# The scores of the attention take their PSUM banks from the tag with four banks instead of the one with two

## Chip, cores and metric

The kernel runs on one core of a Trainium2 chip. The metric is the device time of one execution in microseconds. Three runs of the kernel before gave a median of 1214.59 us (1214.19 to 1215.19). In what follows PE is TensorE, DVE is VectorE, ACT is ScalarE, POOL is GpSimd, and SP is the engine that issues most transfers.

## What is computed

Two layers of a hybrid backbone over 256 latent tokens and 256 context tokens, 1024 wide, in float32. Each layer has a mixer with four parallel branches (pooling, short convolution, attention, a bidirectional Mamba-2 SSD) between one input and one output projection. Then comes a SwiGLU FFN in layer 0 and a mixture of eight experts (MoE) in layer 1. The core of the reference, for one layer:

```python
sh1, sc1, gt1, sh2, sc2, gt2 = split(silu(c) @ w_ada[l] + b_ada[l])
h, hc = rmsnorm(x) * (1 + sc1) + sh1, rmsnorm(xc) * (1 + sc1c) + sh1c
...
o = concatenate([pool_mix(p_pool), short_conv_mix(p_conv),
                 na_attention(q, k, v, kc, vc, rpb), o_ssd])
x = x + gt1 * (o @ w_out[l])
...
def ctx_attention(q, k, v):
    s = jnp.einsum('bqhd,bkhd->bhqk', q, k) * (1.0 / math.sqrt(hd))
    p = jax.nn.softmax(s, axis=-1)
    return jnp.einsum('bhqk,bkhd->bqhd', p, v)
```

The attention has four heads of 64 channels. A latent token attends to latent tokens in a window (with a bias) and to all context tokens; a context token attends to context tokens alone. The context stream is needed out of layer 0 but not out of layer 1, so layer 1 computes the latent half alone.

## The kernel before

The kernel is one program of some 18,000 instructions. A scheduler in the framework decides the order in which each engine runs them. It simulates the program with its own costs (`TCARGS`, L21) and takes the order of the code as priority. Which PSUM bank a tile may have is one of its constraints, so a change of banks can reorder instructions far from the place where it is made. Each engine then works through its own order, and an instruction that waits holds up all that stand behind it on its engine.

PSUM has eight banks of 128 partitions by 512 float32. `PSB` (L25) shares them out to three tags, `g` with four banks, `s` with two and `m` with two. `ps(tag, name)` (L364) takes a tile of one bank from the rotation of its tag. The tag `g` serves the input projections (tiles `g_...`, also the groups of `G4`) and, while a mixer runs, the products `adaps` and `adao` of the modulation vectors. `s` serves the SSD branch (`gram`, `rowbc`, `inter`, `yps`) and `poolps`. `m` serves the transposes of `turn` (L750) and, before the change, the whole attention.

A weight of the projections is split on the way in: `raw` comes from memory, ACT writes its rounded high part `wh` (L284), and DVE the rest `wl` (L287). A projection tile `g_N` is a chain of products with `wh` and `wl` from the same bank. Most products are recorded at the helper's line, L342, so tiles are told apart by their names.

The attention (`attn`, L757) is a generator. Its units are (context or latent, head, half of the queries); layer 0 has 16 of them and layer 1 has 8. It is advanced by `NATT` units (4 in layer 0, 2 in layer 1) for each projection. For a pair of heads, `scores` makes two products of 64 rows of TensorE each, one head on rows 0 to 63, the other on rows 64 to 127, each into a bank of its own:

```python
for i in range(2):
    r = slice(64 * i, 64 * i + 64)
    both.append(self.ps(ATAGS[0], "attS"))
    ms.append(self.mm(both[i][:, :nk], self.qT[r, c, q0:q0 + P], self.kT[r, c, k0:k0 + nk]))
self.inorder(ms)
```

`nk` is 512 for latent queries and 256 for context queries. `stage1` is the softmax on ACT and DVE: for latent units a copy of the context half (L784), the bias `nab` added to the rest (`attsb`, L785), the maximum (L786), the exponential (L787), the reciprocal and the scaling of `attP` (L788, L789); context units go by L780 and L781 instead. `stage2` transposes the probabilities into a bank of tag `ATAGS[1]` (`attT`, L796) and copies them to `PT` on ACT (L797). `pv` multiplies them with the values into a bank of tag `ATAGS[2]` (`attO`), eight products of 64 columns of TensorE for a latent pair and four for a context pair, and `hilo` splits that into `omx` (L399, L400), an input of the output projection.

Other work stands in the same stretches. Pooling copies its projection to `pu` (L690), sums shifted copies on DVE (L696 to L711) and multiplies on TensorE (`poolps`). The SSD makes `decay` (ACT L972, DVE L991) and `xd` (L980) for the products `yps`, adds the `inter` products on DVE (L1006, L1010: `ysb`), gates with `zs` (L1013), normalises (L1015 to L1020) and transposes on TensorE (`ytr`, L1024).

Of the kernel before, what the change touches and what calls it, by code (L numbers as in the profile page):

```python
# [31 lines left out]
OSLOT = ("xst", "Bt", "nab", "zs", None, None, "BT", "CT")  # L32
ADAFILL = (0, 1, 0, 1, 0, 1, 0, 1, 0, 1, 0, 1, 0, 0, 0, 0, 0, 0, 1, 1, 0, 0, 0, 0, 0, 0, 0, 0, 0, 0, 0, 0, 0, 0, 0, 0, 0, 0, 0, 0, 1, 1, 1, 0, 0, 0, 0, 0, 0, 0, 0, 0, 0, 0, 0, 0, 0, 0, 0, 0, 0, 0)
NATT = ((4, 4, 4, 4, 4, 4, 4, 4, 4, 4, 4, 4, 4, 4, 4, 4), (2, 2, 2, 2, 2, 2, 2, 2, 2, 2, 2, 2, 2, 2, 2, 2))
ATAGS = 'mmm'
G4 = 'gggg'
ADAGROUPS = ((0, (4, 5, 6, 7)), (0, (8, 9)), (1, (0, 1)), (1, (4, 5, 6)))

# [217 lines left out]
class Kern:  # L256
# [500 lines left out]
    def attn(self, full):  # L757
        V, A = self.V, self.A

        def scores(ctx, c, qt):  # L760
# [5 lines left out]
# [4 lines that stand above are left out]
# [22 lines left out]
        def stage2(pr, pt, qt):  # L792
            n = pr.shape[-1] // P
            tp = self.ps(ATAGS[1], "attT")
            for c in range(n):
# [21 lines left out]
        def pv(ctx, c):  # L817
            op = self.ps(ATAGS[2], "attO")
            nk = 2 if ctx else 4
            kb = 2 if ctx else 0  # L820
            ms = []
            for k in range(nk):
                for h in (2 * c, 2 * c + 1):
                    r = 64 * (h % 2)
                    ms.append(self.mm(op[r:r + 64, :256], self.vt[:, kb + k, h * 64:h * 64 + 64], pts[ctx, h][:, k, :],
                                      start=k == 0, stop=k == nk - 1))
            self.inorder(ms)
            o0 = 256 * ctx
            self.hilo(self.out(4 + c), slice(o0, o0 + 256), op[:, :256])
# [1194 lines left out]
```

## Time and profile before

| | us |
|---|---|
| median of three runs | 1214.59 (1214.19 to 1215.19) |
| the profiled execution | 1213.07 |
| its span (first to last instruction) | 1211.3 |
| TensorE busy | 1165.6 (96%) |
| VectorE busy | 736.8 (61%) |
| ScalarE busy | 461.1 (38%) |

The stages follow one another: start, mixer of layer 0 (about 70 to 240 us, attention on TensorE from 128), FFN (about 275 to 660), mixer of layer 1 (about 660 to 805, attention from 731), MoE (to the end). A row of the timeline is a run of equal instructions on one engine: start, length, engine, line, operation, what it writes and reads, shape, and how many records it merges (one float32 product of the attention's scores has two). In brackets stands the idle time ahead of it, if there is one, and what ended it. A row's length includes an end that overlaps the next row, so what a run costs is read from the start of the next row.

### The profile page before, as it was taken

Reading aid. Unit: us, or ns where it says so; the run is one execution under the profiler, and the core shown is the slowest. Engines: PE = TensorE matmul, PEld = TensorE weight load, DVE = VectorE, ACT = ScalarE, POOL = GpSimd, SP = SyncE. Lnnn points to the kernel's source line nnn. Section 1 sums busy time; section 2 is a strip of 40 time slices with the busy share of each in tenths; the row PEclk is TensorE's granted clock in tenths of the full one; section 3 lists DMA queues with packets and bytes.
Section 4 is the critical chain, followed back from the end, with each engine's and each line's share of the span. In section 5 each row is a group of like instructions: output and inputs, shape, how many; then the busy total and the mean of one; then the engine's idle time right before and its main releaser. Section 6 shows DMA issues by size and latency. Waiting matters only on the chain. (4 is left out here: it accounts for less than half of the span.)

```text
span 1211.3 us, 17942 instructions
## 1 busy us (share of the span) xinstructions
PE 1165.6 (96%) x6601; PEld 831.0 (69%) x6601; DVE 736.8 (61%) x1612; ACT 461.1 (38%) x863; POOL 8.9 (1%) x30
## 2 busy tenths in 40 slices
PE   6999999999999999999999999988999999999994
PEld 3787676787788888888886897884467534446741
DVE  4554667347979756764336778644588524447942
ACT  4443453324322231232223555541276423435721
POOL 0000000000000000000000000000000000000000
PEclk9999999999999999999999999998999999999997
DMA  9635424229565443543223442276999999896984
GB/s 373 228 138 209 144 83 139 84 87 374 201 206 187 162 155 128 187 154 122 87 101 126 141 139 88 90 252 244 359 401 407 344 401 394 300 409 238 375 286 179
DMA packets 88752, 264.16 MB, mean 218 GB/s; under 512 B 8144, under 2 KB 24144, under 8 KB 88528
## 3 DMA queue, kind: packets, MB, share of 16 engines
q1 hardware_dynamic: 88080, 260.84, 59.1%
q0 software_dynamic: 576, 2.10, 0.5%
q8 instruction: 54, 0.88, 0.3%
q14 instruction: 42, 0.34, 0.1%
HBM read 261.85 MB, written 1.05 MB: 217 GB/s over the span
## 5 line engine op out<-in xcount | busy, mean ns | idle before, releaser
L287 DVE TENSOR_TENSOR wl<-raw,wh 128x512 fp32r<-128x512 f32 (+2 forms) x288 | 257.0, 920 | 108.9 <-ACT wh L284 108.0
L284 ACT ACTIVATE wh<-raw 128x512 fp32r<-128x512 f32 (+2 forms) x288 | 225.4, 815 | 250.6 <-PE dps L342 67.3
L342 PE MATMUL g<-hmix,wh 128*128 128x512 f32 (+1 forms) x640 | 182.3, 364 | 0.3
L342 PEld LDWEIGHTS g<-hmix,wh 128*128 128x128 f32 x640 | 112.3, 189 | 31.6 <-issue 11.3
L342 PE MATMUL gps<-hffn,wh 128*128 128x512 f32 x320 | 125.0, 394 | 0.8 <-DVE gth L1158 0.8
L342 PE MATMUL ups<-hffn,wh 128*128 128x512 f32 x320 | 124.8, 394 | 0.0
L342 PE MATMUL g<-hmix,wl 128*128 128x512 f32 (+1 forms) x320 | 114.9, 359 | 0.0
L342 PE MATMUL dps<-aT,wh 128*128 128x512 f32 x352 | 111.0, 394 | 0.0
L453 DVE SCALAR_TENSOR_TENSOR sprod<-raw,srep 128x1024 f32<-128x1024 f32 x72 | 87.8, 1220 | 26.3 <-DMA raw<-in_adat_dram 25.8
L342 PE MATMUL mgu<-wh,xg 128*128 128x512 f32 (+1 forms) x288 | 89.2, 381 | 0.0
L342 PEld LDWEIGHTS dps<-aT,wh 128*128 128x128 f32 x352 | 66.0, 188 | 15.8
L342 PEld LDWEIGHTS gps<-hffn,wh 128*128 128x128 f32 x320 | 60.4, 189 | 15.4 <-DVE gth L1158 1.2
L342 PEld LDWEIGHTS ups<-hffn,wh 128*128 128x128 f32 x320 | 60.5, 189 | 14.2
L342 PE MATMUL dps<-aT,wl 128*128 128x512 f32 x176 | 69.7, 396 | 0.0
L342 PEld LDWEIGHTS g<-hmix,wl 128*128 128x128 f32 x320 | 60.4, 189 | 8.4 <-issue 1.0
L342 PE MATMUL ups<-hffn,wl 128*128 128x512 f32 x160 | 63.4, 396 | 0.0
L342 PE MATMUL gps<-hffn,wl 128*128 128x512 f32 x160 | 63.4, 396 | 0.0
L342 PEld LDWEIGHTS mgu<-wh,xg 128*128 128x128 f32 x288 | 52.8, 188 | 13.1 <-issue 3.8
L342 PE MATMUL mgu<-wl,xg 128*128 128x512 f32 (+1 forms) x144 | 57.4, 398 | 0.0
L1138 DVE SCALAR_TENSOR_TENSOR xres<-dps,mods,xres 128x256 f32<-128x256 f32 x64 | 27.5, 477 | 28.6 <-PE dps L342 28.4
L1663 DVE SCALAR_TENSOR_TENSOR mth<-mth,mgu 128x256 f32<-128x256 f32 (+1 forms) x30 | 11.5, 394 | 53.2 <-ACT mth L1662 52.8
L342 PE MATMUL mdn<-wh,aT 128*128 128x512 f32 x132 | 43.5, 400 | 0.0
(396 smaller groups left out, 1820.1 us busy)
## 6 DMA issues: line engine op xcount, KB each, us to landing
raw<-in_mg_dram SPq DMA_DIRECT2D x141, 512.0 KB, 6.7
raw<-in_md_dram SPq DMA_DIRECT2D x76, 512.0 KB, 7.5
raw<-in_ada_dram SPq DMA_DIRECT2D x60, 512.0 KB, 4.1
raw<-in_fg_dram SPq DMA_DIRECT2D x44, 512.0 KB, 4.2
raw<-in_wi_dram SPq DMA_DIRECT2D x40, 512.0 KB, 4.3
raw<-in_adat_dram SPq DMA_DIRECT2D x36, 512.0 KB, 3.3
xres<-in_mg_dram SPq DMA_DIRECT2D x23, 512.0 KB, 7.5
raw<-in_fd_dram SPq DMA_DIRECT2D x22, 512.0 KB, 3.3
```

The lines of the kernel that those rows point to most:

```text
L284: up = self.A.activation(h, src, AF.Copy)
L287: sub = self.V.tensor_tensor(lo, src, h.bitcast(F32), op=OP.subtract)
L342: return self.E.matmul(out, l, r, start=start, stop=stop, skip_group_check=True)
L453: V.scalar_tensor_tensor(y, t[:, :1024], 1.0, s[:, j], op0=OP.mult, op1=OP.mult, accum_out=o[:, q, j:j + 1])
L1138: self.V.scalar_tensor_tensor(self.x[:, d, s], ps[:, s], gt[:, j:j + 1], self.x[:, d, s], op0=OP.mult, op1=OP.add)
L1663: V.scalar_tensor_tensor(th, th, 1.0, p[:, :hw], op0=OP.add, op1=OP.mult)
```

## The change

The letter for the scores goes from `m` to `g`; the transposed probabilities and the output stay in `m`.

```diff
--- before.py
+++ after.py
@@ -32,7 +32,7 @@
 OSLOT = ("xst", "Bt", "nab", "zs", None, None, "BT", "CT")
 ADAFILL = (0, 1, 0, 1, 0, 1, 0, 1, 0, 1, 0, 1, 0, 0, 0, 0, 0, 0, 1, 1, 0, 0, 0, 0, 0, 0, 0, 0, 0, 0, 0, 0, 0, 0, 0, 0, 0, 0, 0, 0, 1, 1, 1, 0, 0, 0, 0, 0, 0, 0, 0, 0, 0, 0, 0, 0, 0, 0, 0, 0, 0, 0)
 NATT = ((4, 4, 4, 4, 4, 4, 4, 4, 4, 4, 4, 4, 4, 4, 4, 4), (2, 2, 2, 2, 2, 2, 2, 2, 2, 2, 2, 2, 2, 2, 2, 2))
-ATAGS = 'mmm'
+ATAGS = 'gmm'
 G4 = 'gggg'
 ADAGROUPS = ((0, (4, 5, 6, 7)), (0, (8, 9)), (1, (0, 1)), (1, (4, 5, 6)))
```

The scheduler makes another order of it. On TensorE it is the same up to the first pair of the attention in layer 0, and differs in many places behind that, also in FFN and MoE. Three places follow, each before and then after. Numbers of buffers are left out except where a name has one; `x4` is four instructions.

TensorE, layer 0, directly behind the first pair of scores; `adaps` is a product for the modulation vectors. Before:

```order
L342 MATMUL yps<-xd,decay 128x64 x7
L342 MATMUL adaps<-raw,s_98 32x512 x4
L342 MATMUL attS<-kT,qT 128x512
L342 MATMUL adaps<-raw,s_98 32x512 x4
L342 MATMUL g_1466<-hmix,wh 128x512
```

After:

```order
L342 MATMUL yps<-xd,decay 128x64 x7
L342 MATMUL adaps<-raw,s_98 32x512 x2
L342 MATMUL attS<-kT,qT 128x512 x2
L342 MATMUL adaps<-raw,s_98 32x512 x6
L342 MATMUL gram<-CT,BT 128x128 x2
L796 MATMUL attT<-constp,attP 128x128 x4
L342 MATMUL g_1466<-hmix,wh 128x512
```

A later score product has moved up next to another one, and the transposes follow before the next projection g_1466.

TensorE, layer 0, from the end of the projection g_1755, whose result goes to pooling, to g_1868. Before:

```order
L342 MATMUL g_1755<-hmix,wh 128x512
L342 MATMUL inter<-hin,CT 128x256 x2
L342 MATMUL adaps<-raw,s_98 32x512 x4
L342 MATMUL yps<-xd,decay 128x64
L342 MATMUL attS<-kT,qT 128x256
L342 MATMUL yps<-xd,decay 128x64 x7
L342 MATMUL attS<-kT,qT 128x256
L342 MATMUL adaps<-raw,s_98 32x512 x4
L342 MATMUL poolps<-pp,layerv 128x512
L342 MATMUL g_1868<-hmix,wh 128x512
```

After:

```order
L342 MATMUL g_1755<-hmix,wh 128x512
L796 MATMUL attT<-constp,attP 128x128 x4
L342 MATMUL adaps<-raw,s_98 32x512 x6
L342 MATMUL attO<-PT,vt 64x256 x4
L342 MATMUL poolps<-pp,layerv 128x512
L342 MATMUL attS<-kT,qT 128x256 x3
L1024 MATMUL ytr<-constp,zs 128x128 x8
L342 MATMUL attS<-kT,qT 128x256
L342 MATMUL g_1868<-hmix,wh 128x512
```

`inter` and `yps` have moved forward, into the projection; transposes and `attO` stand ahead of `poolps`, three of four score products behind it, and then `ytr`.

TensorE, layer 1, from the end of g_6073 to g_6165. Before:

```order
L342 MATMUL g_6073<-hmix,wh 128x256
L342 MATMUL attS<-kT,qT 128x512
L342 MATMUL rowbc<-constr 128x512
L342 MATMUL rowbc<-constr,la_5705 128x128 x8
L342 MATMUL attS<-kT,qT 128x512
L342 MATMUL inter<-hin,CT 128x256 x2
L342 MATMUL yps<-xd,decay 128x64
L796 MATMUL attT<-constp,attP 128x128 x4
L342 MATMUL yps<-xd,decay 128x64 x7
L796 MATMUL attT<-constp,attP 128x128 x4
L342 MATMUL poolps<-pp,layerv 128x256
L342 MATMUL g_6165<-hmix,wh 128x256
```

After:

```order
L342 MATMUL g_6073<-hmix,wh 128x256
L342 MATMUL rowbc<-constr 128x512
L342 MATMUL rowbc<-constr,la_5705 128x128 x8
L796 MATMUL attT<-constp,attP 128x128 x4
L342 MATMUL inter<-hin,CT 128x256 x2
L342 MATMUL yps<-xd,decay 128x64 x8
L796 MATMUL attT<-constp,attP 128x128 x4
L342 MATMUL poolps<-pp,layerv 128x256
L342 MATMUL attS<-kT,qT 128x512 x2
L342 MATMUL g_6165<-hmix,wh 128x256
```

The two single score products are no longer between the `rowbc` and the `yps`; a pair of them stands behind `poolps`.

## Rows read from the trace of the kernel before

**Rows 1.** The page, part 1: busy us of each engine, share of the span, instructions.

```profile
PE 1165.6 (96%) x6601; PEld 831.0 (69%) x6601; DVE 736.8 (61%) x1612; ACT 461.1 (38%) x863; POOL 8.9 (1%) x30
```

**Rows 2.** Stretches: busy (instructions) of PE, PEld, DVE, ACT, POOL; PE's clock; DMA; GB/s.

```profile
360.00:390.00 30.00, 30.00 (x131) 24.24 (x130) 24.23 (x42) 6.26 (x6) 0.00 (x0) 1.00 0.50 168
...
1190.00:1198.00 8.00, 5.84 (x30) 2.13 (x31) 1.90 (x4) 0.20 (x1) 0.00 (x0) 0.79 0.24 89
```

**Rows 3.** Waits of PE: total us, times, longest.

```profile
PE attT L796 <- DVE attsb L785: 1.0, 1, 1.0
...
PE g L342 <- ACT omx L399: 0.5, 1, 0.5
```

**Rows 4.** Timeline of PE, single score products (layer 0) and a pair (layer 1).

```profile
127.87 0.39 PE L342 MATMUL g<-hmix,wh 128*128 128x512 f32 x1
128.19 1.12 PE L342 MATMUL attS<-kT,qT 64*128 64x512 f32 x2
129.24 0.43 PE L342 MATMUL yps<-xd,decay 128*128 128x64 f32 x2
...
731.22 1.13 PE L342 MATMUL attS<-kT,qT 64*128 64x512 f32 x4
732.28 0.38 PE L342 MATMUL g<-hmix,wh 128*128 128x256 f32 x1
732.50 0.28 PE L342 MATMUL g<-hmix,wl 128*128 128x256 f32 x1
732.62 0.40 PE L342 MATMUL g<-hmix,wh 128*128 128x256 f32 x2
```

**Rows 5.** Timeline of PE, layer 0, around the pooling products.

```profile
160.92 1.00 PE L342 MATMUL rowbc<-constr,la 128*128 128x128 f32 x8
...
167.54 1.12 PE L796 MATMUL attT<-constp,attP 128*128 128x128 f32 x8
...
182.29 1.03 PE L342 MATMUL inter<-hin,CT 128*128 128x256 f32 x4
183.25 1.07 PE L342 MATMUL adaps<-raw,s 128*32 128x512 f32 x8
...
184.61 0.70 PE L342 MATMUL attS<-kT,qT 64*128 64x256 f32 x2
185.23 1.77 PE L342 MATMUL yps<-xd,decay 128*128 128x64 f32 x14
...
188.56 1.13 PE L342 MATMUL poolps<-pp,layerv 128*128 128x512 f32 x2
...
192.63 1.95 PE L342 MATMUL attO<-PT,vt 128*64 128x256 f32 x16
```

**Rows 6.** Timeline of ACT and DVE behind g_1755.

```profile
182.49 0.59 ACT L690 COPY pu<-g 128x512 f32<-128x512 f32 x1 [0.63 <-PE g L342]
...
183.18 0.72 DVE L696 TENSOR_TENSOR psum<-pu 128x542 f32<-128x542 f32 x1
...
186.46 0.69 DVE L711 TENSOR_TENSOR pp<-pp,pu 128x512 f32<-128x512 f32 x1
...
187.46 1.21 DVE L287 TENSOR_TENSOR wl<-raw,wh 128x1024 fp32r<-128x1024 f32 x1
```

**Rows 7.** Timeline of DVE behind g_1612, first and last pooling step.

```profile
161.59 0.72 DVE L696 TENSOR_TENSOR psum<-pu 128x542 f32<-128x542 f32 x1 [0.21 <-ACT pu L690]
...
169.04 0.68 DVE L711 TENSOR_TENSOR pp<-pp,pu 128x512 f32<-128x512 f32 x1
```

**Rows 8.** Timeline of PE, layer 1, behind g_6073.

```profile
742.64 1.77 PE L342 MATMUL yps<-xd,decay 128*128 128x64 f32 x14 [0.60 <-DVE decay L991]
```

**Rows 9.** Timeline of DVE, layer 1, behind g_6073.

```profile
741.91 0.68 DVE L991 TENSOR_TENSOR decay<-decay,gram 128x512 f32<-128x512 f32 x1
```

**Rows 10.** Timeline of PE in the MoE, two idle times.

```profile
1142.70 0.50 PE L342 MATMUL mdn<-wl,aT 128*128 128x512 f32 x1 [1.65 <-DVE wl L287]
...
1191.50 4.48 PE L342 MATMUL mdn<-raw,aTw 128*32 128x512 f32 x24 [2.24 <-DMA raw<-in_md_dram]
```

## Prediction

> **What bounds the kernel now.** I read the busy shares first. TensorE is busy for 96% of the span [rows 1], so the attention counts by what it takes of TensorE's row and by the holes it makes there. The list of waits, and the timeline where a wait stands in brackets, give the holes in the stretches with attention: 1.0 us (transposes attT, for softmax), 0.5 (a projection, for omx) [rows 3] and 0.60 (yps, for decay) [rows 8]. So nearly all of the attention's TensorE time is on the path that sets the end.
>
> Then the timeline of TensorE, tile by tile. A score product uses 64 of the 128 rows. One head's 512-column product, which the trace shows as x2, starts at 128.19, and the next tile starts at 129.24: 1.05 us. Where both heads of a pair stand next to each other, x4 in the trace, they start at 731.22 and the next tile at 732.28: 1.06 us for both [rows 4]. The two heads use the two row halves at the same time. **A head that stands alone costs as much as a pair.** Before, all 16 score products of layer 0 stand alone; in layer 1 two pairs are together and four products are alone. The code gives the reason: the scores of both heads, the transposed probabilities and the output share two banks, so the second product waits for a bank that softmax or a copy holds.
>
> **What the change takes away.** By the changed order (the pieces above show three places) the heads come together in two of the four latent pairs of layer 0: 2 x 1.05 = 2.1 us. In layer 1 six visits become four: 2.1 us. The context scores have 256 columns; one alone takes 0.62 (184.61 to 185.23) [rows 5]. They now come as three and one, twice. In each three, the second is hidden behind the first, and I let the third, which is on the first one's row half, cost a full 0.62; the fourth stands alone. That hides two of eight: 1.3 us. Together **-5.5 us**; the bound is nothing, if neighbours in this order don't overlap (third rival).
>
> **Fewer visits.** Before a score product the last projection step takes 0.32 us (127.87 to 128.19), and the first 256-column step behind one 0.22 (732.28 to 732.50) [rows 4]. Inside a projection a step is 0.23 for 512 columns (131 in 30 us) [rows 2] and 0.12 for 256 (732.50 to 732.62) [rows 4]. That is 0.1 at each end, 0.2 a visit. Visits by scores go from 16 to 10 in layer 0 and from 6 to 4 in layer 1: 8 x 0.2 = 1.6. The output products attO, 1.95 us for eight in a row [rows 5], are now cut by another tile at three places: 0.6 back. **-1.0 us**, with bounds of -1.6 (cuts are free) and +0.6 (visits are free and cuts are not). The Trainium skill, page TensorEngine Tiling (Array Packing), Key Properties, says that a change of tiling mode drains TensorE; the steps of 0.32 and 0.22 agree, and no term rests on the page.
>
> **What it moves: the cover.** The lone score products stood where TensorE would have waited for VectorE or ScalarE anyway. The changed order also pulls inter and yps of the SSD branch forward, into the projections. Three places lose cover.
>
> Place A, layer 0, behind the projection g_1612. poolps waits for the pooling sums on VectorE. Before, from the projection's end (rowbc follows it, 160.92 less its first step of 0.22) to the last pooling step (169.04 + 0.68) [rows 5, 7] are 9.0 us, filled by scores, attO, yps and transposes without a hole. In the changed order TensorE has eight transposes (1.1), eight yps (2.0, by 1.77 for seven), eight attO with a gram between (2.3) and nine rowbc (1.2) ahead of poolps, and no scores: 6.6 us [rows 5]. VectorE's row there loses a softmax step and gets some of the SSD's; I estimate its chain at 8.1 to 9.0. Hole 1.5 to 2.4; I take **+1.9**, in part at rowbc, whose bank the ysb updates free. Bounds 0.5 and 3.
>
> Place B, layer 0, behind g_1755. Before, inter, adaps, yps and scores fill the time from 182.29 to poolps at 188.56 [rows 5]. The chain that they hide: the copy pu on ScalarE at 182.49, then VectorE from 183.18 to 187.15 [rows 6], 4.9 us after the projection's end. In the changed order TensorE has only four transposes (0.5), six adaps (1.6, by 1.07 for four) and four attO (1.0) there: 3.1 us [rows 5]. And the chain grows. VectorE gets a weight step among the pooling steps (L287, 1.21 us [rows 6]), small steps of a norm, and an omx step that waits for attO itself; without the softmax step that goes, I estimate 6.1 us. Hole 3.0, some of it before attO, most before poolps. Behind poolps comes ytr, which waits for the norm that ends last on VectorE: 0.9 more. **+3.9**. Bounds 2.0 (the weight step runs earlier) and 5.5. Queued behind poolps on TensorE are three scores, ytr and all of the next projection.
>
> Place C, layer 1, behind g_6073. Before, two lone score products stand there around rowbc, and yps still waits 0.60, until 742.64 [rows 8], for the decay product that VectorE ends at 742.59 [rows 9]. Without the two TensorE is there 2.1 us sooner. The decay product comes perhaps 0.5 to 1.0 sooner, because that pair's attsb and attP steps leave VectorE's row. So yps waits some 2.0 instead of 0.60, and I take **+1.6** with an edge for xd behind it; bounds +0.5 and +2.1.
>
> **Waits that go.** The 0.5 for omx goes, because attO no longer stands in front of that group. The 1.0 before attT [rows 3] becomes about 0.6, since a pair's softmax starts sooner. **-0.9**.
>
> **Sum.** -5.5 - 1.0 + 1.9 + 3.9 + 1.6 - 0.9 = 0.0 us. FFN and MoE get some swapped rows, but the same work, and TensorE is full in them (30.00 of 30 us in the stretch from 360 [rows 2]); I cost that at nothing, and at most 1 us either way, the largest wait of [rows 3]. The profiled execution took 1213.07, 1.5 below the median of 1214.59; against the median the sum gives **1214.6 us**. A measurement of this kernel can tell about 0.2%, 2.4 us, from no change.
>
> The Trainium skill speaks against the change: TensorEngine Tiling (Array Packing), PSUM Bottleneck, says that packing speeds up TensorE but not the reading of its banks, which may become the limit. Places A to C would be that here; the trace of before shows it only in the waits of [rows 3, 8].
>
> **Rivals.** First, faster: with softmax no longer held up by banks, VectorE and ScalarE run ahead and the lost cover isn't missed. A and C cost nothing, of B only its 2.0 stays: -5.5 - 1.0 - 0.9 + 2.0 = -5.4, **1209.2**. For it: VectorE is busy for 61% of the span and ScalarE for 38% [rows 1]. Against it: the pooling chain can't start before its projection ends, and poolps stands ahead of the scores on TensorE. The page Perfetto Trace Analysis of the Trainium skill, Matmuls, has the rule for this rival: independent groups should rotate through different banks, so that evacuation overlaps the next group's products. No run here shows yet which of the two holds.
>
> Second, slower: the clock. At 1191.50 TensorE has been idle for 2.24 us [rows 10], and over the 8 us around that the mean granted clock is 0.79 [rows 2], a part of it at the lower level of 1.2 GHz: 0.21 x 8 = 1.7 us lost. At 1142.70 it has been idle for 1.65 [rows 10] and goes on in steps of the full 2.4 GHz. B has a hole of up to 3.0 and C one of 2.0. If the clock falls at both, 3.4 us come on top: **1218.0**, slower by 0.28%. It decides from a hole as long as the first of these. At one place alone it is 1216.3, within 0.2%.
>
> Third, it doesn't do what it says: the heads are neighbours in the order, but the second waits for its bank, since projections in flight use the same four. All 5.5 is lost: **1220.1**. Against it: the pairs of [rows 4] overlap with two banks already.
>
> **How the numbers follow.** The forecast, with everything that ends within 0.2%, gets 0.44, the first rival 0.30, the second 0.20, the third 0.06. So faster 0.30, same 0.44, slower 0.26. The range goes from the first rival to a little above the second, with 1 us for the upper bounds of A and B: 1209.5 to 1219. The forecast's own is 1212.2 to 1217.0.
>
> **What would show it.** Scores in 14 visits instead of 22, and all four pairs of layer 1 at 1.05 us. TensorE's waits should list poolps for a pooling step on VectorE (L711) at 2 us or more, and yps for decay (L991) near 2. If poolps waits for less than 1 us, B is wrong and the result is faster. A lower granted clock in layer 0's or layer 1's attention shows the second rival; 2.1 us for a pair of neighbours shows the third.

## The result, and the profile after

The changed kernel takes **1222.88 us** (median of four, 1222.12 to 1223.64) against 1214.89 us for the kernel before, measured on the same chip. The ratio is 1.0063, with a 95% interval of 1.0047 to 1.0079. It is slower by 0.6%, 8 us, where no measurable change was forecast, and it lies above the range (1209.5 to 1219).

One statement ahead of the prediction is wrong, and the result turns on it. The text on the kernel before puts `poolps` into tag `s`. The code has it in tag `g` (L713), the tag into which the change puts the scores.

The page of the changed kernel, beside [rows 1]:

```profile
span 1221.0 us, 17949 instructions
...
PE 1168.4 (96%) x6601; PEld 833.7 (68%) x6601; DVE 736.7 (60%) x1612; ACT 460.6 (38%) x863; POOL 9.4 (1%) x30
```

TensorE has the same number of matmul records, 6601, and is busy for 2.8 us more, though fewer score products stand alone. The span is 9.7 us longer. Its parts, from the starts of the same rows in both traces: 0.9 us before the first score product, where TensorE's order is the same in both; 3.7 from there to the first norm behind the mixer of layer 0 (145.59 before, 149.25 after); 0.8 from there to the FFN; nothing in the FFN; 2.2 in layer 1 from the first score to the router (68.70, 70.88); 2.1 behind that, in router and MoE.

The waits of TensorE in the changed kernel (total us, times, longest), for [rows 3]:

```profile
PE poolps L342 <- DVE pp L711: 3.9, 2, 3.1
...
PE yps L342 <- ACT decay L972: 1.2, 2, 0.9
...
PE yps L342 <- DVE decay L991: 0.9, 1, 0.9
PE rowbc L342 <- DVE ysb L1010: 0.6, 1, 0.6
```

Place A is 0.56 us at `rowbc` and 0.78 at `poolps`, place B is 3.13 at `poolps`, place C is 0.88 and 0.86 at `yps`. These are the three places of the prediction. The two waits that it took away (`omx` and `attsb`) are gone; a new one of 0.34, not forecast, stands at a later `yps` in layer 1.

Place B in the timeline of TensorE, for [rows 5]:

```profile
193.25 1.08 PE L342 MATMUL attO<-PT,vt 128*64 128x256 f32 x8
197.47 2.08 PE L342 MATMUL poolps<-pp,layerv 128*128 128x512 f32 x2 [3.13 <-DVE pp L711]
199.47 1.74 PE L342 MATMUL attS<-kT,qT 64*128 64x256 f32 x6
201.14 1.09 PE L1024 MATMUL ytr<-constp,zs 128*128 128x128 f32 x8
```

And what VectorE does meanwhile, for [rows 6]:

```profile
192.29 0.71 DVE L696 TENSOR_TENSOR psum<-pu 128x542 f32<-128x542 f32 x1
...
194.35 1.21 DVE L287 TENSOR_TENSOR wl<-raw,wh 128x1024 fp32r<-128x1024 f32 x1
...
196.40 0.42 DVE L400 TENSOR_TENSOR omx<-attO,omx 128x256 fp32r<-128x256 f32 x1
196.73 0.68 DVE L711 TENSOR_TENSOR pp<-pp,pu 128x512 f32<-128x512 f32 x1
```

The weight step and the omx step stand among the pooling steps, as the changed order has them. The last pooling step ends at 197.41, and `poolps` starts. It then takes 2.0 us (to 199.47), and the three scores behind it take 1.67. At place A of the same trace, equal products take 1.05 and 1.06:

```profile
175.46 1.12 PE L342 MATMUL poolps<-pp,layerv 128*128 128x512 f32 x2 [0.78 <-DVE pp L711]
176.51 1.13 PE L342 MATMUL attS<-kT,qT 64*128 64x256 f32 x6
177.57 0.50 PE L342 MATMUL rowbc<-constr 128*128 128x512 f32 x1
```

At place B TensorE runs at the lower clock. Place C shows the same, beside [rows 8]:

```profile
745.59 0.43 PE L342 MATMUL yps<-xd,decay 128*128 128x64 f32 x2 [0.88 <-ACT decay L972]
746.88 3.25 PE L342 MATMUL yps<-xd,decay 128*128 128x64 f32 x14 [0.86 <-DVE decay L991]
749.93 1.06 PE L796 MATMUL attT<-constp,attP 128*128 128x128 f32 x4
...
751.77 2.07 PE L342 MATMUL attS<-kT,qT 64*128 64x512 f32 x4
```

Seven `yps` take 3.05 us (before: 1.61), a pair of scores 2.00 (before: 1.06). Stretches of the changed kernel, columns as in [rows 2]:

```profile
195.00:205.00 10.00, 7.53 (x28) 4.63 (x29) 8.42 (x25) 3.25 (x9) 0.00 (x0) 0.83 0.54 196
...
745.00:765.00 20.00, 18.18 (x107) 14.16 (x107) 14.76 (x37) 9.73 (x28) 2.16 (x2) 0.83 0.23 79
```

The granted clock is 0.83 over 10 and over 20 us: 0.17 x 10 = 1.7 us and 0.17 x 20 = 3.4 us lost. In the same stretches before it was 1.00. But the kernel before has low stretches of its own elsewhere, ahead of the FFN and in the MoE:

```profile
276.00:282.00 6.00, 6.00 (x39) 2.95 (x42) 2.66 (x14) 0.19 (x1) 0.00 (x0) 0.72 1.01 401
1192.00:1196.00 4.00, 3.98 (x24) 0.73 (x16) 0.00 (x0) 0.00 (x0) 0.00 (x0) 0.57 0.04 14
```

They cost 0.28 x 6 = 1.7 and 0.43 x 4 = 1.7 us. In the same places of the changed kernel (281 to 287 and 1202 to 1206) the clock is 1.00, although the second has a longer wait ahead of it than before, 3.15 us instead of 2.24 [rows 10]:

```profile
1202.62 2.97 PE L342 MATMUL mdn<-raw,aTw 128*32 128x512 f32 x24 [3.15 <-DMA raw<-in_md_dram]
```

So over the whole span the clock cost the changed kernel some 1.7 us more than the kernel before, and 5.1 us more in the two attentions.

The last piece is in the rows of the narrow products, where the changed order cuts a group. Timeline of TensorE, layer 0:

```profile
133.28 1.05 PE L342 MATMUL adaps<-raw,s 128*32 128x512 f32 x4
134.26 1.13 PE L342 MATMUL attS<-kT,qT 64*128 64x512 f32 x4
135.32 1.91 PE L342 MATMUL adaps<-raw,s 128*32 128x512 f32 x12
137.16 0.71 PE L342 MATMUL gram<-CT,BT 128*128 128x128 f32 x4
...
153.34 0.65 PE L342 MATMUL attO<-PT,vt 128*64 128x256 f32 x2
153.92 0.83 PE L342 MATMUL adao<-constp,adaev 128*128 128x8 f32 x6
154.68 1.52 PE L342 MATMUL attO<-PT,vt 128*64 128x256 f32 x12
156.13 0.71 PE L342 MATMUL gram<-CT,BT 128*128 128x128 f32 x4
```

The trace has two records for each of these products. Two `adaps` take 0.98 us (133.28 to 134.26) and the six behind them 1.84 (135.32 to 137.16). Before, a run of four is one row of 1.07 [rows 5], and the six runs of four take 5.97 in all. An `adaps` uses 32 of the 128 columns of the array, and four neighbours run side by side: a group of two costs as much as one of four. One `attO` on 64 columns takes 0.58 alone; six take 1.45, 0.48 for a pair.

Time of TensorE by tile, from the start of a row to the start of the next, waits apart, in us; layer 0 from the first score to the norm, layer 1 from the first score to the router. The kernels e4, e5 and e7 come below.

| | before | after | e4 | e5 | e7 |
|---|---|---|---|---|---|
| layer 0: scores attS | 13.41 | 10.33 | 9.69 | 10.09 | 8.86 |
| attO | 5.86 | 7.23 | 8.20 | 8.20 | 8.39 |
| adaps | 5.97 | 7.36 | 7.37 | 8.48 | 7.50 |
| projections g | 92.62 | 90.64 | 91.21 | 91.60 | 91.11 |
| poolps | 1.52 | 3.05 | 1.36 | 1.32 | 2.01 |
| all else | 25.57 | 26.17 | 26.61 | 25.91 | 25.92 |
| waits | 0.64 | 4.47 | 0.00 | 0.00 | 0.00 |
| sum | 145.59 | 149.25 | 144.44 | 145.60 | 143.79 |
| layer 1: sum | 68.70 | 70.88 | 66.11 | 69.05 | 65.81 |
| of it waits | 1.63 | 2.08 | 0.00 | 0.00 | 0.00 |

### The profile page after: what moved, and what is told of

It is laid out like the page before. It is cut to its first block, busy times and chain, and to the rows that moved or that the text cites. A ratio compares the mean times of both kernels' runs of the same rounds, so it can differ in the third digit from the quotient of the medians.

```text
span 1221.0 us, 17949 instructions
## 1 busy us (share of the span) xinstructions
PE 1168.4 (96%) x6601; PEld 833.7 (68%) x6601; DVE 736.7 (60%) x1612; ACT 460.6 (38%) x863; POOL 9.4 (1%) x30
## 3 DMA queue, kind: packets, MB, share of 16 engines
HBM read 261.85 MB, written 1.05 MB: 215 GB/s over the span
## 5 line engine op out<-in xcount | busy, mean ns | idle before, releaser
L342 PE MATMUL g<-hmix,wh 128*128 128x512 f32 (+1 forms) x640 | 179.4, 361 | 0.3
L342 PE MATMUL mgu<-raw,xgw 128*32 128x512 f32 (+1 forms) x340 | 44.6, 557 | 0.0
```

Of the source, the lines that this page charges most:

```text
L342: return self.E.matmul(out, l, r, start=start, stop=stop, skip_group_check=True)
```

## Experiments

The ratios are to the kernel before, which was measured beside each group of runs (medians 1214.06 us for e1 to e4, 1214.92 for e5 to e7, 1214.44 for e8).

**The theory.** In the changed order the 84 projection and score tiles of tag g have their first product on TensorE in exactly the order in which the code takes them, none out of turn, and the four of `poolps` keep that turn too; so do the 60 projection tiles of tag g and the 66 tiles of tag m before. A tile takes its bank in turn within its tag, with its first product. `poolps` takes a bank of tag g, and its first product is also its only one, which waits for the pooling sums. Before, only the next projection stood behind it in that tag, and the scores, in tag m, could pass it. By the order one score product did so at place A, and two at each of the two `poolps` of layer 1. At place B none did: the two ahead of `poolps` there belong to earlier units, and come earlier in the changed order. With the change the next scores are in the same tag and have to stand behind `poolps`: at all four places they follow it directly. The rivals were that the cut groups cause the loss, that tag g has too few banks, and that the loss is in one layer or in the MoE.

**e1 and e2, one layer at a time.** The edit, from the changed kernel:

```diff
-                both.append(self.ps(ATAGS[0], "attS"))
+                both.append(self.ps("g" if full else "m", "attS"))
```

This is e1, since `full` is true in layer 0; e2 has the two letters exchanged.

> Only the scores of layer 0 take their banks from tag g; those of layer 1 stay in m. Main theory (tag order): tiles of one tag get their first product in the order of the code, so scores in g queue behind poolps and no longer fill the wait for the pooling sums; the holes let the clock fall. Then layer 0 is as in the changed kernel, about 3.7 us later at its end than before plus 0.8 at the start of the FFN, and layer 1 and the MoE take as long as before: 1218.5 to 1219.5 us against 1214.9. Rival (the loss is elsewhere, in the reordered MoE): layer 0 costs little by itself, within 1.5 us of before.

> Only the scores of layer 1 take their banks from tag g. Main theory: yps waits for decay as in the changed kernel (0.9 + 0.9 us), the clock falls behind it, layer 1 is 2.2 us longer, and the one MoE group of eight 32-column products that is cut into seven and one costs 1 to 2 us more: 1218 to 1219 us. Rival (removal of the lone products is a net gain in layer 1, and its loss in the changed kernel came from layer 0): 1213 us or less.

Measured: e1 takes 1221.89 us, ratio 1.0056 (1.0039 to 1.0074), above its forecast; e2 takes 1215.61, ratio 1.0011 (1.0001 to 1.0021), between its forecast and its rival. Most of the loss is layer 0's. In e2 layer 1 is 2.16 us longer, as expected, but router and MoE together are some 1.6 us shorter than in the profiled execution of before. The products `mgu` do take 1.6 us more there, but the products `mdn` take 1.6 less; 1.5 of that is the last group, which ran at the lower clock before (4.47 us) and not in e2 (2.97). In e1 layer 0 is 8.2 us longer and not 3.7, with the same order of TensorE there as in the changed kernel and nearly the same waits (0.56, 0.77, 3.28). Stretches of e1 and then of the changed kernel tell why:

```profile
174.00:178.00 4.00, 3.50 (x9) 1.53 (x9) 1.94 (x4) 2.66 (x9) 0.00 (x0) 0.64 0.01 2
178.00:182.00 4.00, 4.00 (x14) 3.15 (x13) 2.24 (x8) 2.44 (x10) 0.00 (x0) 0.51 0.00 0
...
195.00:205.00 10.00, 6.72 (x25) 3.26 (x22) 8.85 (x25) 2.66 (x7) 0.00 (x0) 0.70 0.71 262
```

```profile
174.00:178.00 4.00, 3.23 (x18) 1.90 (x16) 2.69 (x7) 2.68 (x9) 0.00 (x0) 1.00 0.01 2
178.00:182.00 4.00, 4.00 (x31) 2.21 (x31) 3.21 (x11) 2.63 (x11) 0.00 (x0) 1.00 0.00 0
```

In e1 the clock falls behind place A too, after waits of 0.56 and 0.77 us with some work between; in the changed kernel it doesn't, after the same waits. What a wait costs through the clock thus differed between two executions with the same order in this stretch. The loss by low clock in layer 0 is 1.7 us in the one trace and 0.36 x 4 + 0.49 x 4 + 0.30 x 10 = 6.4 in the other.

**e3, the scores ahead of poolps in the code.** `evac_pool` keeps its VectorE steps and returns the rest, which the mixer calls behind the units of the attention:

```diff
-                self.evac_pool(name, p, n)
+                late = self.evac_pool(name, p, n)
...
                 next(units, None)
+            if name[0] == "p":
+                late()
             fill()
```

> The change, and one more: poolps and its two readers stand behind the units of the attention in the code instead of ahead of them. The tag stays g. In the kernel before this edit alone changes no place of TensorE's order around the pooling. Main theory (tag order): scores come ahead of poolps again, TensorE's waits for pooling steps and decay fall from 6.2 us to under 2, the clock does not fall in either attention, and the time comes down by 6 to 9 us from the changed kernel: 1214 to 1217 us. Rival (cut groups: adaps 2-6-8-5-3, attO 1-6-1 and 1-7, are what the change costs): the cuts are still there, so the time stays at 1220 us or more.

Measured: 1218.80 us, ratio 1.0042 (1.0027 to 1.0056): the right way, but by 4.1 us between the medians (2.6 by the ratios) instead of 6 to 9. The waits of TensorE (its lines from L713 on are three further down):

```profile
PE attT L799 <- DVE attP L792: 1.5, 1, 1.5
...
PE attT L799 <- ACT PT L800: 1.0, 2, 0.5
PE rowbc L342 <- DVE ysb L1013: 0.9, 1, 0.9
```

`poolps` has left the list, and layer 0 takes 145.60 us, as before the change. In place of the old waits stand shorter ones for softmax. Layer 1 still has 2.04 us of waits, the clock still falls there, and router and MoE are 3.4 us longer than before. That the order decides in layer 0 is confirmed, with the cuts (adaps 7.49, attO 7.65) still in.

**e4 and e7, poolps in another tag.** One word each, at L713:

```diff
-        q = self.ps("g", "poolps")
+        q = self.ps("m", "poolps")
```

This is e4; e7 has "s".

> The change, and poolps takes its bank from tag m instead of g. Main theory: neither scores nor the next projection queue behind poolps; the holes at poolps vanish (under 0.3 us), no clock loss in layer 0, 1212 to 1215 us. attO is cut at more places (1-6-1, 1-7, 1-3, 1-3 in layer 0, 1-7 twice in layer 1) and adaps 2-6-10-6, so rival (cut groups decide): 1219 us or more.

> The change with poolps in tag s, that of gram, rowbc, inter and yps. Four context pairs of layer 0 are together instead of three and one twice. Main theory: scores are free of poolps as in tag m; if poolps in s makes the SSD branch queue for the pooling sums instead, yps or rowbc waits appear, but the projections fill them: 1206 to 1211 us. Rival (cuts of attO, 1-6-1, 1-7, 1-3, 1-2-1, and adaps 2-6-8-6-2 decide): over 1214 us.

Measured: e4 **1207.53 us**, ratio 0.9940 (0.9924 to 0.9957); e7 **1208.15 us**, ratio 0.9940 (0.9922 to 0.9958). Both beat both kernels: 0.6% faster than before, 15 us faster than the changed kernel. For e4 that is more than the theory had forecast. Stretches of e4:

```profile
125.00:205.00 80.00, 80.00 (x446) 56.03 (x446) 56.16 (x147) 38.15 (x102) 3.07 (x8) 1.00 0.39 131
...
725.00:805.00 80.00, 79.72 (x599) 70.30 (x598) 58.66 (x146) 43.69 (x97) 1.48 (x4) 1.00 0.36 124
```

TensorE has no wait in the attention of either layer, and the clock stays up. `poolps` now stands inside the next projection. The cuts are there in full (attO 8.20 and 8.39, adaps 7.37 and 7.50 in the table), so the rival that they decide falls. The gain is not all in the attentions, though. Of the 13.9 us between the profiled executions of the changed kernel and e4, 4.8 lie in layer 0, 4.8 in layer 1 and 4.3 in router and MoE, of which the theory says nothing; between the kernel before and e4 it is 1.2, 2.6 and 2.3 us. The theory is shown for the two attentions. The rest comes with the scheduler's other order behind them, and no run separates it.

**e5, the bank taken early.** The tag stays g, and `poolps` waits as late as ever:

```diff
         q = self.ps("g", "poolps")
+        self.mm(q[:, 0:8], self.lyv("poolw")[:, 0:P], self.cst("ident")[:, 0:8])
```

> The change, and ahead of each poolps one product of 8 columns into the same bank that waits for nothing (the real product overwrites it). poolps stays in tag g and as late as it is. Main theory (the scores queue only for poolps' turn to take a bank): once the small product has taken the bank, scores and the next projection pass, the waits for pooling steps vanish from TensorE (under 0.3 us), the clock stays up in layer 0, and the time falls by 5 to 10 us from the changed kernel to 1208 to 1215. Rival (shortage of banks in g: projections, adaps, poolps and scores need more than four): the bank is now held longer, so the time stays at 1219 or rises.

Measured: 1214.46 us, ratio 0.9990 (0.9981 to 1.0000). Four products of eight columns, which nobody reads, take 0.7% off the changed kernel. Stretches:

```profile
125.00:205.00 80.00, 80.00 (x443) 54.48 (x442) 52.78 (x142) 39.94 (x106) 3.08 (x8) 1.00 0.37 125
```

No wait, no low clock. The rival (too few banks) is not the cause of the loss. It may be a reason why e5 stays behind e4: with a bank held longer, in layer 1 only the first pair stays together, and adaps is cut to 2-6-10-1-1-4 (8.48 us). That was not tested; layer 1 is 2.9 us longer than in e4, and router and MoE are 3.0 longer.

**e6, poolps alone.** The kernel before with the edit of e4, scores in m:

> The kernel before with poolps in tag m; the scores stay in m, so nothing of the change is in it. It tells whether the gain of the change with poolps in m (1207.5) comes from poolps alone. Main theory (both are needed: the change pairs the heads, poolps out of g gives the cover back): no pairs here, the next projection may pass poolps but there was nearly no hole to fill, and adaps is cut to 4-4-1-4-2-1-2-6, three more groups at about 0.9 us: 1214 to 1218 us. Rival (poolps alone does it): 1207 to 1210 us.

Measured: 1219.09 us, ratio 1.0042 (1.0025 to 1.0059), a little above what the theory allowed. The gain of e4 needs both edits. This kernel also gives the price of a cut by itself. Timeline of TensorE:

```profile
162.43 1.05 PE L342 MATMUL adaps<-raw,s 128*32 128x512 f32 x2
163.41 0.50 PE L342 MATMUL rowbc<-constr 128*128 128x512 f32 x1
...
164.68 1.06 PE L342 MATMUL adaps<-raw,s 128*32 128x512 f32 x8
165.67 1.13 PE L342 MATMUL inter<-hin,CT 128*128 128x256 f32 x4
...
169.66 1.05 PE L342 MATMUL adaps<-raw,s 128*32 128x512 f32 x4
170.65 0.43 PE L342 MATMUL yps<-xd,decay 128*128 128x64 f32 x2
```

One, four and two products take 0.98, 0.99 and 0.99 us. By its order (4-4-1-4-2-1-2-6) it has nine groups where before had six, and its adaps take 8.76 us instead of 5.97: 2.79 for three, 0.93 each. Also longer in layer 0 are the waits, by 1.5 us at attO and for omx, and the projections, by 1.6, which more visits interrupt; that these visits are the reason is an argument. Other rows are shorter, and layer 0 is 5.0 us longer in all.

**e8, work in the hole.** Three products into the bank of `poolps` at place B, which wait only for the second pooling step, and the context scores tied behind the real `poolps`, so that the order at B stays:

```diff
+        if n == 2 and i == 0:
+            for _ in range(FILL):
+                self.mm(q[:, :n * 256], self.lyv("poolw")[:, 0:P], sums[1][:, :, 8:264])
+        self.poolmm = self.mm(q[:, :n * 256], self.lyv("poolw")[:, i * P:i * P + P], p.rearrange("p s t -> p (s t)"))
...
-            self.inorder(ms)
+            self.inorder(([self.poolmm] if full and self.poolmm else []) + ms)
```

`FILL` is 3.

> The change, and in layer 0, place B, three products of 512 columns into poolps's bank that wait only for the second pooling step; the real poolps overwrites them. The scores of the context units are tied behind the real poolps, so that they don't profit from the taken bank: TensorE's order at B is attT, adaps, attO, the three, poolps, three scores, ytr, one score, as in the changed kernel but for the three. The wait for the pooling sums stays, but TensorE works in it. Theory (the hole costs twice, once as idle time and once by the clock that falls behind it): poolps starts as late as before (3 us after attO), but poolps, three scores and ytr run at 2.4 GHz, about 1.05, 1.06 and 0.8 us; layer 0 is about 1.7 to 2 us shorter than in the changed kernel's profiled execution (149.25 us from the first score to the norm). Rival (the slow stretch behind the wait has another cause, such as banks or operands): poolps and the scores take twice as long as elsewhere here too, and layer 0 stays at 149 us or gets longer by what the three products overrun.

Measured: 1218.10 us, ratio 1.0024 (1.0010 to 1.0037). Timeline of TensorE at place B (lines are one further down):

```profile
194.57 2.84 PE L343 MATMUL poolps<-psum,layerv 128*128 128x512 f32 x6
197.98 1.13 PE L343 MATMUL poolps<-pp,layerv 128*128 128x512 f32 x2 [0.56 <-DVE pp L712]
199.03 1.13 PE L343 MATMUL attS<-kT,qT 64*128 64x256 f32 x6
200.09 1.09 PE L1028 MATMUL ytr<-constp,zs 128*128 128x128 f32 x8
```

`poolps` starts 3.4 us behind the start of the three, as late as ever, and then takes 1.05 us, the three scores 1.06. The granted clock of the stretch is 1.00:

```profile
198.00:202.00 4.00, 3.45 (x17) 2.05 (x18) 3.74 (x12) 1.57 (x4) 0.00 (x0) 1.00 0.61 251
```

The rival is out: with the same banks and operands, `poolps` and the scores run at full speed. That the filled wait is what kept the clock up is likely and not shown by one execution, since the clock behind equal waits differs anyway (e1). The forecast for the stretch missed all the same: layer 0 takes 149.44 us, not 147.4. There is a wait of 0.55 before the last score, the next attO is cut 1-3 (7.87 us instead of 7.23), and other rows are a little longer. The lower total beside the changed kernel comes from behind layer 0: layer 1, with the same waits, lost less by the clock (69.34 instead of 70.88), and norm and MoE were shorter. That part is chance of the clock or of small order changes, and e8 shows no more than its rows at B.

## Why the prediction was wrong

**What bounds the kernel** was right. All that moved is on TensorE's row.

**Scores, -5.5.** In layer 0 the scores take 3.1 us less, 3.7 when the 0.6 of low clock behind place B is taken off; -3.4 was forecast. In layer 1 all four pairs take 1.06 at full clock, as forecast. The heads do overlap; the third rival is out. Two slips of the working changed nothing: 2 x 0.62 is 1.2 and not 1.3, and the range, said to start at the first rival's 1209.2, starts at 1209.5.

**Visits and cuts, -1.0.** This term failed. The visits gave more than thought: projections are 2.0 us shorter in layer 0 and 1.0 in layer 1. The cuts cost far more. I priced a cut as one more visit, 0.2, and only for attO. What is lost is the neighbour: attO takes 1.37 more in layer 0 and 0.48 in layer 1, adaps 1.39 more. That is 3.2 us instead of 0.6. The changed order of adaps, 2-6, stood in a fence ahead of the prediction. [rows 5] shows four adaps in 1.07 us, about what one lone score product takes; I did not read that row as a group. In the MoE a group of eight `mgu` is cut to seven and one, another microsecond; I had costed the MoE at nothing, because it does the same work, and the same work in another order is not the same time.

**Places A, B, C, +7.4.** The waits were nearly right in size: A 1.34 (1.9), B 3.13 (3.0 in `poolps` and attO), C 1.74 instead of 0.60 before (1.6 more was forecast, 1.1 came). The 0.9 at ytr did not appear, nor did it in e8, where TensorE came to ytr at full clock. That the waits are a rule of the tag and not an accident of this order, I did not see, because I had `poolps` in the wrong tag. The changed order has scores directly behind every `poolps`; I used it against the first rival and did not ask why.

**The clock** is the step that failed most. I named it as the second rival, with its place and its mechanism, gave it 0.20 and put it at nothing in the sum. It fell at B and at C: 1.7 + 3.4 = 5.1 us instead of the 3.4 I gave for both. The condition, a hole as long as 2.24 us, does not hold either way: C waited 0.88 and 0.86 with 0.4 us of work between, about the 1.65 behind which the clock had stayed up, and e1 shows it falling even behind 0.56 and 0.77; behind the 3.15 in the changed kernel's MoE it stayed up.

**Sum.** Between the two profiled executions the three things left out are 5.1 for the clock at B and C, 3.2 - 0.6 = 2.6 for the cuts and 2.1 for router and MoE: 9.8 us against a span that is 9.7 longer where 0.0 was forecast. That these two agree so closely is in part luck. What else was off nearly cancels: visits gave 1.4 us more than thought, the scores 0.3, the waits that go 0.4, and ytr (0.9), place A (0.6) and place C (0.5) cost less; against that stand 0.9 us before the first score, 0.8 at the norms, and about 2 us in `poolps` and the other rows. And the 0.8 at the norms and the 2.1 in router and MoE are net of the 1.7 us each that the kernel before lost there by its own low clock.

**Open.** The 2.1 us in router and MoE are 2.0 more in the `mgu` (one lone product accounts for 1.0), 1.2 more in waits for the transfers of the last weights, 0.6 in other rows, and 1.7 less in the `mdn`, where the clock stayed up. Why the transfers came later was not tried. The same stretch differs by up to 5.9 us among the kernels here (e1 shortest, e3 longest), and by how much in equal programs was not measured. Why the clock falls behind equal waits in one execution and not in another is not settled either.

**What was cited.** The Trainium skill's TensorEngine Tiling (Array Packing), PSUM Bottleneck, was named as speaking against the change. The change was slower, but not for that reason: VectorE and ScalarE did the same work (736.7 and 460.6 us), and TensorE waited behind a tile that had its bank and not yet its input (3.13 us at place B). The Trainium skill's Perfetto Trace Analysis, Matmuls, on rotation through banks, agrees with e4 and e7, where nothing late stands in the rotation of the scores: TensorE has no wait in either attention.

## What to carry to other kernels

Before a tile moves to another tag, list what else takes a bank there and when its first product can start: a tile whose only product waits long holds up everything behind it in the tag. The additional banks paid only together with taking that tile out (e4, e7); giving it an early first product (e5) made up for the loss, and taking it out without the banks (e6) gained nothing. Narrow products earn their packing only as neighbours, so count groups and not products in the new order. And price an idle stretch of TensorE as the wait plus what the clock may take behind it: at B and C that was 5.1 us for 4.9 us of waits, at A nothing (in e1 3.4 us), and behind the 3.15 us in the MoE nothing.

## What the runs showed of the hardware

I had not expected three things. One, two or four 32-column products of 512 columns take the same time (0.98 to 1.00 us, e6). The granted clock fell to the lower level behind waits of 0.9 and 0.9 us with work of 0.4 between (3.4 us lost in layer 1); behind 0.56 and 0.78 it stayed up in one execution, and behind 0.56 and 0.77 it fell in another; and it stayed up behind a wait of 3.15 us. And behind a wait in which TensorE did useless work (e8) the next rows ran at full clock, in the one execution that was profiled.
